# A Mamba-2 and attention trunk: the products inside the chunks in one run per group, and dt's projection in plain fp32 column tiles

## The chip, the cores and the metric

One core of one Trainium2 chip runs the whole kernel. The metric is the device time of one execution in microseconds (us). TensorE multiplies matrices, VectorE (DVE), ScalarE (ACT) and GpSimd (POOL) do the elementwise work, and SyncE (SP) issues nearly all transfers.

## The reference

The input is one sequence of 512 tokens with 1024 features, in float32. Two layers follow each other, then a final RMS norm.

```
# layer 1: Mamba-2 mixer (8 groups of 4 heads, head dim 64, state 128)
h = rms_norm(x, norm_g);  zxbcdt = h @ w_in          # z 2048, x/B/C 4096, dt 32 columns
xbc = silu(causal_depthwise_conv(xbc))               # 4 taps
dt = softplus(dt_raw + dt_bias);  adt = -exp(a_log) * dt
# scan, in chunks:
acs = cumsum(adt);  decay = exp(acs[l] - acs[s]) for s <= l
y_diag = (C B^T * decay) @ (x * dt)                  # the products inside the chunk
y_off  = (C @ state) * exp(acs)                      # what earlier chunks left
y = y_diag + y_off + d_skip * x
y = group_rms_norm(y * silu(z)) * g;  x = x + y @ w_out
# shared K/V of x; layer 2: differential attention (8 heads, two softmax maps each,
# ALiBi, block-causal mask), gate, out projection, residual; final RMS norm
```

## The kernel before

Everything is float32. The large projections are made of three fp32r products each (high part by high part, high by low, low by high), so that every weight and every activation is first split into a rounded high part (`whi`, `a_hi`: ScalarE) and the rest (`wlo`, `a_lo`: VectorE). Smaller products (the scan, the transposes, attention's weighted sums) are plain fp32, which the trace shows as two TensorE instructions for each product.

The sequence is cut into four chunks of 128 tokens (`NQ = NT = 4`). The mixer goes through the groups g = 0 to 7. For each group `group_proj(g)` makes B, C and x (`pg`, 96 products of 512 columns, then `conv`), and `ssd(g)` does the scan:

- `pcb`: C times B for each chunk, into the one bank of the tag "long"; four VectorE products multiply it into `dec`, the decays of the four heads.
- `psA`, `psB`: the states that the chunks leave (`hst`).
- `pyd`: the products inside the chunks. `pyd{g}_0` holds chunks 0 and 1, `pyd{g}_1` chunks 2 and 3. Each of their 32 products has 64 weight columns (half of a chunk's rows, slices 0:64 and 64:128 of the output) and 64 moving columns. VectorE then adds each half into `dx`, which holds the skip term.
- `po1`, `po2`: what the earlier states give, then the gate with z, the group norm (`rsqrt`), the transposes `pyt`, and the split of y into `yh` and `yl` for the output projection.

TensorE's accumulators come from three rings of banks: "mm" (4 banks, the projections), "ss" (3 banks: psA, psB, pyd, po1, po2, the transposes and ps_dt) and "long" (1 bank: pcb, the 1/rms product, later the attention outputs).

The work is traced in this order: the setup with the first half of z's first tile, the row norm `scales` (the 1/rms of every token, as a column and, by one product of a matrix of ones with diagonals that POOL makes, as a row `ar_row`), dt's projection and softplus, the decays, and then the stream `z0 g0 g1 z1 g2 g3 z2 g4 o0 g5 z3 g6 g7 o1 o2 o3` with `ssd(g)` after each g. In this mixer part a planner at build time orders each engine's instructions, by a list of priorities (those traced earlier first) and its own estimate of times: when the inputs of an instruction are late, later work takes its place. At run time every engine goes through its list in order. An instruction that is recorded while `T.on` (or `V.on`, `A.on`) is set is pinned behind the one traced before it on its engine. From the last output projection on (`last_rows`, then attention) everything is pinned, so the order there is the written one.

`dt` before the change: for each of the 8 blocks of 128 features the 32 weight columns are scaled by the norm's gain and split into a high and a low part (`dw`, written twice side by side, 128 columns), and multiplied with the high and the low part of the input (`hh`, `hl`), 512 tokens at once: 16 fp32r products into `ps_dt`. ScalarE and VectorE add the two halves and lay the four token chunks under each other (`pre`), and VectorE multiplies by `r_row`, the row of 1/rms.

Nearly every TensorE, VectorE and ScalarE instruction is issued through the helper `Ordered.call`, which is why the profile shows L55 for it; the groups are told apart by the names of their tiles.

Of the kernel before, what the change touches and what calls it, by code (L numbers as in the profile page):

```python
# [9 lines left out]
F32 = mybir.dt.float32  # L10
F32R = mybir.dt.float32r
I32 = mybir.dt.int32
AF = mybir.ActivationFunctionType
ALU = mybir.AluOpType
# [3 lines left out]
P = 128  # L18
# [3 lines left out]
KD = D // P  # L22
G = 8
R = 4
HD = 64
H = 32
NQ = 4
# [11 lines left out]
C_GA, C_GK, C_GB, C_GG, C_SG, C_DTB, C_AL, C_CB, C_CW = 0, 8, 16, 24, 40, 41, 42, 43, 75  # L39
# [24 lines left out]
def trunk(ctx, tc, x, x_t, par, w_dt, w_in, w_out, w_kvqg, w_bo, d_skip, lam_qk, fin_g, out):  # L64
    nc = tc.nc
    V, A, T = (Ordered(tc, e) for e in (nc.vector, nc.scalar, nc.tensor))
# [14 lines left out]
    def ss_bank(name):  # L81
        turns[0] += 1
        tag = "mm" if turns[0] % turns[1] >= 3 else "ss"
        return psum.tile([P, 512], F32, tag=tag, name=name, bufs=3 if tag == "ss" else 4)

    def long_bank(name):
        return psum.tile([P, 512], F32, tag="long", name=name)
# [10 lines left out]
    prm = const.tile([P, C_CB], F32, name="prm")  # L98
# [142 lines left out]
    def rsqrt(v, n, tag, bufs=2):  # L241


        y = small.tile([P, n], F32, tag=f"{tag}_y", name=f"{tag}_y", bufs=bufs)
        c = small.tile([P, n], F32, tag=f"{tag}_c", name=f"{tag}_c", bufs=bufs)
        iy = small.tile([P, n], I32, tag=f"{tag}_i", name=f"{tag}_i", bufs=bufs)

        def vyy():
            if n == 1:
                V.scalar_tensor_tensor(out=c, in0=y, scalar=v, in1=y, op0=ALU.mult, op1=ALU.mult)  # L250
            else:
                V.tensor_tensor(out=c, in0=y, in1=v, op=ALU.mult)
                V.tensor_tensor(out=c, in0=c, in1=y, op=ALU.mult)

        V.tensor_scalar(out=iy, in0=v.bitcast(I32), scalar1=1, scalar2=None, op0=ALU.logical_shift_right)
        V.tensor_scalar(out=y.bitcast(I32), in0=iy, scalar1=-1.0, scalar2=float(0x5F3759DF - 2 ** 31), op0=ALU.mult, op1=ALU.add)
        vyy()
        V.scalar_tensor_tensor(out=c, in0=c, scalar=-10.0 / 3.0, in1=c, op0=ALU.add, op1=ALU.mult)
        V.scalar_tensor_tensor(out=y, in0=c, scalar=5.0, in1=y, op0=ALU.add, op1=ALU.mult)
        vyy()  # L260
        V.scalar_tensor_tensor(out=y, in0=c, scalar=-64.0 / 3.0, in1=y, op0=ALU.add, op1=ALU.mult)
        return y
# [39 lines left out]
    def scales(tag, ss):  # L302

        V.tensor_scalar(out=ss, in0=ss, scalar1=ROOT2 / D, scalar2=ROOT2 * EPS, op0=ALU.mult, op1=ALU.add)
        col = res.tile([P, NT], F32, tag="r_col", name=f"{tag}r_col")
        V.tensor_copy(col, rsqrt(ss, NT, "y"))
        w = small.tile([P, NT + 1, P], F32, tag="wide", name=f"{tag}diag", bufs=2)
        GP.memset(w[:, NT], 1.0)
        for t in range(NT):
            GP.tensor_tensor(out=w[:, t], in0=ident, in1=col[:, t:t + 1].to_broadcast([P, P]), op=ALU.mult)  # L310
        ps = long_bank(f"{tag}ps_r")
        T.matmul(ps, lhsT=w[:, NT], rhs=w[:, 0:NT].rearrange("p t n -> p (t n)"), start=True, stop=True)
        row = res.tile([P, S], F32, tag="r_row", name=f"{tag}r_row")
        A.copy(row, ps)
        return col, row
# [14 lines left out]
    def new_h(tag):  # L330
        return [res.tile([P, KD, S], F32R, tag=f"hT_{i}", name=f"{tag}_{i}") for i in ("hi", "lo")]
# [9 lines left out]
    hh, hl = new_h("a")  # L341
# [4 lines left out]
    bp2 = bctx.enter_context(tc.tile_pool(name="bp2", bufs=2))  # L346
# [17 lines left out]
    xt = [bp2.tile([P, 2, S], F32, tag="yl", name=f"xt{i}", bufs=4) for i in range(4)]  # L364
# [27 lines left out]
    for t in range(NT):  # L392
        squares(ss, t)
    r_col, r_row = scales("a", ss)
    V.tensor_scalar(out=sg1, in0=prm[:, C_SG:C_SG + 1], scalar1=0.5 * (1.0 - LAM0), scalar2=None, op0=ALU.mult)
    dtw_raw = sm.tile([P, KD, H], F32, name="dtw_raw")
# [1 line left out]

    dw = bp2.tile([P, KD, 2, 2, H], F32R, tag="yh", name="dw", bufs=4)
    for k in range(KD):
        src = dtw_raw[:, k, :].unsqueeze(1).to_broadcast([P, 2, H])
        gk = prm[:, C_GA + k:C_GA + k + 1]
        A.activation(dw[:, k, :, 0], src, AF.Copy, scale=gk)
        V.scalar_tensor_tensor(out=dw[:, k, :, 1], in0=src, scalar=gk, in1=dw[:, k, :, 0].bitcast(F32), op0=ALU.mult, op1=ALU.subtract)
    ps_dt = ss_bank("ps_dt")
    for k in range(KD):
        w = dw[:, k].rearrange("p a b h -> p (a b h)")
        T.matmul(ps_dt, lhsT=w, rhs=hh[:, k, :], start=k == 0, stop=False)  # L410
        T.matmul(ps_dt, lhsT=w, rhs=hl[:, k, :], start=False, stop=k == KD - 1)

    pre = sm.tile([P, P], F32, name="pre")
    for c in range(NQ):
        sl, hi, lo = (slice(i * H, (i + 1) * H) for i in (c, 0, 1))
        cs = slice(c * P, (c + 1) * P)
        A.copy(pre[sl, :], ps_dt[lo, cs])
        V.tensor_tensor(out=pre[sl, :], in0=ps_dt[hi, cs], in1=pre[sl, :], op=ALU.add)
    for c in range(NQ):
        sl = slice(c * H, (c + 1) * H)  # L420
        V.tensor_tensor(out=pre[sl, :], in0=pre[sl, :], in1=r_row[sl, c * P:(c + 1) * P], op=ALU.mult)
    V.tensor_scalar(out=pre, in0=pre, scalar1=prm[:, C_DTB:C_DTB + 1], scalar2=None, op0=ALU.add)
    e1 = sm.tile([P, P], F32, name="e1")
    A.activation(e1, pre, AF.Abs)
# [136 lines left out]
    def ssd(g):  # L561
        bc, cc, x0, x1 = conv_out.pop(g)
        xc = (x0, x1)
        dec, een, _ = decs.pop(g)
# [3 lines left out]
        for c in range(NQ):  # L568
            cs = slice(c * P, (c + 1) * P)
# [8 lines left out]
        for j in range(2):  # L578
            pxt = ss_bank(f"pxt{g}_{j}")
            for c in range(NQ):  # L580
# [5 lines left out]
                            in1=dsk[:, h2].unsqueeze(1).unsqueeze(3).to_broadcast([P, NQ, 2, HD]), op=ALU.mult)  # L586
# [6 lines left out]
        hst = bp.tile([P, 3, R, HD], F32, tag="hst", name=f"hst{g}")  # L593
        hsf = hst.rearrange("p c h e -> p c (h e)")
        psA = ss_bank(f"psA{g}")
        for c in range(2):
            T.matmul(psA[:, c * 256:(c + 1) * 256], lhsT=bt[:, c, :], rhs=xe[:, c].rearrange("p h e -> p (h e)"), start=True, stop=True)
        A.copy(hsf[:, 0], psA[:, 0:256])
# [6 lines left out]

        ss4 = small.tile([P, NQ], F32, tag="ss4", name=f"ss4{g}")
        tmp = bp.tile([P, NQ, R, HD], F32, tag="tmp", name=f"tmp{g}")
        pyd = []
        for q in range(2):
            pyd.append(ss_bank(f"pyd{g}_{q}"))  # L610
            for c in (2 * q, 2 * q + 1):
                for h in range(R):
                    o = (c % 2) * 256 + h * HD

                    for r in (slice(0, 64), slice(64, 128)):
                        T.matmul(pyd[q][r, o:o + HD], lhsT=dec[:, h, c, r], rhs=xdt[:, c, h, :], start=True, stop=True)
            dq = dx[:, 2 * q:2 * q + 2].rearrange("p c h e -> p c (h e)")
            V.tensor_tensor(out=dq, in0=pyd[q].rearrange("p (c e) -> p c e", c=2), in1=dq, op=ALU.add)
        if g % 2 and g < G - 1:
# [5 lines left out]
        for c in (2, 3):  # L625
            T.matmul(po2[:, (c - 2) * 256:(c - 1) * 256], lhsT=cc[:, c * P:(c + 1) * P], rhs=hsf[:, c - 1], start=True, stop=True)
        V.tensor_tensor(out=tmp[:, 1], in0=po1[:, 256:512].rearrange("p (h e) -> p h e", e=HD),
                        in1=eacs_tok[:, 1, hs].unsqueeze(2).to_broadcast([P, R, HD]), op=ALU.mult)
        V.tensor_tensor(out=tmp[:, 2:4], in0=po2.rearrange("p (c h e) -> p c h e", h=R, e=HD),
                        in1=eacs_tok[:, 2:4, hs].unsqueeze(3).to_broadcast([P, 2, R, HD]), op=ALU.mult)  # L630
# [12 lines left out]
        yh = bp2.tile([P, 2, S], F32R, tag="yh", name=f"yh{g}", bufs=4)  # L643
# [11 lines left out]
    for g in range(G):  # L655
        until(f"g{g}")
        if g < G - 1:
            ssd(g)
        else:
            with tc.high_priority():  # L660
                ssd(g)
# [3 lines left out]
    hh, hl = new_h("b")  # L665
# [273 lines left out]
    def half(t, n):  # L939
        hs = slice(n * 512, (n + 1) * 512)  # L940
        return x_tok[:, t, hs], fg[:, hs], ot[t][:, hs], out[t * P:(t + 1) * P, hs]
# [59 lines left out]
    h = DH - 1  # L1001
# [59 lines left out]
    y, f, o, dst = half(3, 0)  # L1061
# [71 lines left out]
```

## Time and profile before

| | us |
|---|---|
| median of 3 runs | 729.46 (729.12 to 731.79) |
| profiled execution, its own time | 729.15 |
| its span, first to last instruction | 727.0 |
| TensorE matmul busy | 713.5 (98%) |
| VectorE busy | 528.0 (73%) |
| ScalarE busy | 433.7 (60%) |
| GpSimd busy | 117.7 (16%) |
| granted TensorE clock | 0.998 |

A row of the profile names the line, the engine, the operation, the tile it writes and those it reads, the shape, the count (x32), and the times. "PEld" is the load of weights into TensorE. In the order of time a row gives its start and the time to the end of its last instruction; in the chain of waits each piece has its start and the time that it held up the end. The mixer part lasts until about 440 us, attention from there to the end.

### The profile page before, as it was taken

Reading aid. Unit: us, or ns where it says so; the run is one execution under the profiler, and the core shown is the slowest. Engines: PE = TensorE matmul, PEld = TensorE weight load, DVE = VectorE, ACT = ScalarE, POOL = GpSimd, SP = SyncE. Lnnn points to the kernel's source line nnn. Section 1 sums busy time; section 2 is a strip of 40 time slices with the busy share of each in tenths; the row PEclk is TensorE's granted clock in tenths of the full one; section 3 lists DMA queues with packets and bytes.
Section 4 is the critical chain, followed back from the end, with each engine's and each line's share of the span. In section 5 each row is a group of like instructions: output and inputs, shape, how many; then the busy total and the mean of one; then the engine's idle time right before and its main releaser. Section 6 shows DMA issues by size and latency. Waiting matters only on the chain.

```text
span 727.0 us, 10819 instructions
## 1 busy us (share of the span) xinstructions
PE 713.5 (98%) x3989; PEld 593.1 (82%) x3989; DVE 528.0 (73%) x1202; ACT 433.7 (60%) x965; POOL 117.7 (16%) x158
## 2 busy tenths in 40 slices
PE   9999999999999999999999999999999999999996
PEld 7787888888888888887788869888988898889874
DVE  4688964979479668569995846657667857785886
ACT  5948573654735527527534348667766756756566
POOL 0108241412315024150110101000000000000002
PEclk9999999999999999999999999999999999999999
DMA  8634313314133231231122310331221131122003
GB/s 302 233 131 162 116 59 117 117 58 175 58 117 116 95 137 60 91 142 59 59 70 105 116 59 9 117 115 59 94 82 58 59 117 59 59 90 85 29 1 115
DMA packets 12916, 70.86 MB, mean 97 GB/s; under 512 B 1728, under 2 KB 2496, under 8 KB 5312
## 3 DMA queue, kind: packets, MB, share of 16 engines
q1 hardware_dynamic: 12576, 69.90, 26.5%
q8 instruction: 31, 0.51, 0.3%
q10 hardware_dynamic: 288, 0.28, 0.1%
q14 instruction: 21, 0.17, 0.1%
HBM read 68.02 MB, written 2.16 MB: 97 GB/s over the span
## 4 chain that ended last, share of the span: by engine, by line
PE 90%; DVE 7%; ACT 1%; issue 1%; POOL 0%; ACTq 0%; DVEq 0%; POOLq 0%
PE pg L55 21%; PE po L55 14%; PE pz L55 12%; PE pt L55 7%; PE pv L55 6%; PE pq L55 6%; PE pk L55 6%; PE pb L55 3%; PE sc L55 3%; PE pyd L55 2%; PE pc L55 2%; DVE wlo L55 2%; DVE xc L55 2%; PE pyt L55 1%; PE pxt L55 1%; PE psA L55 1%
## 5 line engine op out<-in xcount | busy, mean ns | idle before, releaser
L55 DVE SCALAR_TENSOR_TENSOR wlo<-raw,prm,whi 128x512 fp32r<-128x512 f32 (+1 forms) x256 | 150.4, 633 | 52.7 <-ACT whi L55 51.3
L55 ACT ACTIVATE whi<-raw,prm 128x512 fp32r<-128x512 f32 (+1 forms) x256 | 136.8, 606 | 81.4 <-PE pg L55 30.1
L55 PE MATMUL pg<-a_hi,whi 128*128 128x512 f32 x256 | 103.3, 404 | 1.5 <-DVE y_c L55 1.5
L55 PE MATMUL pg<-a_hi,wlo 128*128 128x512 f32 x256 | 102.3, 402 | 0.0
L55 PE MATMUL pg<-a_lo,whi 128*128 128x512 f32 x256 | 102.3, 400 | 0.0
L55 DVE SCALAR_TENSOR_TENSOR xc<-pg,prc,xc 128x511 f32<-128x511 f32 (+2 forms) x96 | 69.6, 738 | 4.8 <-ACT xc L55 4.4
L55 PEld LDWEIGHTS pg<-a_hi,whi 128*128 128x128 f32 x256 | 48.1, 188 | 13.1 <-issue 1.9
L55 PEld LDWEIGHTS pg<-a_hi,wlo 128*128 128x128 f32 x256 | 48.1, 188 | 11.0
L55 PEld LDWEIGHTS pg<-a_lo,whi 128*128 128x128 f32 x256 | 48.1, 188 | 10.7
L55 PE MATMUL po<-whi,yh 128*128 128x512 f32 x128 | 51.4, 402 | 1.5 <-DVE xc L55 0.8
L55 PE MATMUL po<-wlo,yh 128*128 128x512 f32 x128 | 51.1, 399 | 0.0
L55 PE MATMUL po<-whi,yl 128*128 128x512 f32 x128 | 50.4, 398 | 0.0
L55 PE MATMUL pz<-wlo,a_hi 128*128 128x512 f32 x128 | 50.3, 399 | 0.0
L55 PE MATMUL pz<-whi,a_lo 128*128 128x512 f32 x128 | 49.8, 398 | 0.0
L55 PE MATMUL pz<-whi,a_hi 128*128 128x512 f32 x128 | 49.6, 401 | 0.0
L971 POOL TENSOR_TENSOR ot<-ot,fg 128x512 f32<-128x512 f32 x4 | 5.1, 1289 | 256.9 <-ACT ot L55 256.9
L55 ACT ACTIVATE s<-s,mx 128x128 f32<-128x128 f32 (+3 forms) x64 | 35.5, 556 | 9.6 <-DVE mx L55 9.1
L55 ACT ACTIVATE xc<-pg,prc 128x512 f32<-128x512 f32 x32 | 24.6, 773 | 26.6 <-DVE pg L55 26.5
L589 POOL TENSOR_TENSOR xe<-xdt,tok 128x256 f32<-128x256 f32 x24 | 17.3, 749 | 139.6 <-DVE xdt L55 139.6
L55 DVE CUSTOM_DVE_ANT_0 s<-sc,bias 128x128 f32<-128x128 f32 (+3 forms) x64 | 29.4, 488 | 12.2 <-PE sc L55 11.7
L55 ACT ACTIVATE xc<-xc 128x512 f32<-128x512 f32 x32 | 20.0, 629 | 28.3 <-DVE xc L55 28.2
L55 PE MATMUL pv<-whi,b_hi 128*128 128x256 f32 x128 | 36.6, 286 | 0.0
(243 smaller groups left out, 1719.7 us busy)
## 6 DMA issues: line engine op xcount, KB each, us to landing
raw<-in_w_in SPq DMA_DIRECT2D x23, 1024.0 KB, 4.8
raw<-in_w_kvqg SPq DMA_DIRECT2D x16, 1024.0 KB, 4.8
dec<-acs_d SPq DMA_DIRECT2D x8, 1024.0 KB, 4.8
raw<-in_w_out SPq DMA_DIRECT2D x8, 1024.0 KB, 4.8
raw<-in_w_bo SPq DMA_DIRECT2D x4, 1024.0 KB, 4.8
x_tok<-in_x SPq DMA_DIRECT2D x4, 512.0 KB, 9.3
out<-ot SPq DMA_DIRECT2D x7, 256.0 KB, 2.4
raw<-in_w_in SPq DMA_DIRECT2D x4, 256.0 KB, 5.8
```

Of the source, the lines that this page charges most:

```text
L55: i = op(*args, **kw)
L589: GP.tensor_tensor(out=xe[:, c], in0=xdt[:, c], in1=toe_tok[:, c, hs].unsqueeze(2).to_broadcast([P, R, HD]), op=ALU.mult)
L971: GP.tensor_tensor(out=o, in0=o, in1=f, op=ALU.mult)
```

## The change

There are two parts.

In `ssd(g)`, `T.on` is set from psA to the end of pyd, so that psA, psB and the 64 products of pyd keep their order. The second half's accumulator is taken from "long" instead of "ss". The second half is computed first, each chunk's heads in reverse, and the two VectorE adds come after both halves in the trace.

For dt, the raw weights are scaled by the gain in one VectorE product (128x256, in place), and multiplied in plain fp32 with the unsplit input `xt`: for each of the 8 feature blocks four products, one for each token chunk, with 32 weight columns and 128 moving columns, each into its own 32 rows of `ps_dt`. So the chunks come out under each other, and the halves need not be added. The 1/rms product and these 32 products are pinned in this order.

```diff
         ps = long_bank(f"{tag}ps_r")
+        T.on = True
         T.matmul(ps, lhsT=w[:, NT], rhs=w[:, 0:NT].rearrange("p t n -> p (t n)"), start=True, stop=True)
+        T.on = False
...
-    dw = bp2.tile([P, KD, 2, 2, H], F32R, tag="yh", name="dw", bufs=4)
+
+    V.tensor_tensor(out=dtw_raw, in0=dtw_raw, in1=prm[:, C_GA:C_GA + KD].unsqueeze(2).to_broadcast([P, KD, H]), op=ALU.mult)
+    ps_dt = ss_bank("ps_dt")
+    T.on = True
     for k in range(KD):
-        src = dtw_raw[:, k, :].unsqueeze(1).to_broadcast([P, 2, H])
-        gk = prm[:, C_GA + k:C_GA + k + 1]
-        A.activation(dw[:, k, :, 0], src, AF.Copy, scale=gk)
-        V.scalar_tensor_tensor(out=dw[:, k, :, 1], in0=src, scalar=gk, in1=dw[:, k, :, 0].bitcast(F32), op0=ALU.mult, op1=ALU.subtract)
-    ps_dt = ss_bank("ps_dt")
-    for k in range(KD):
-        w = dw[:, k].rearrange("p a b h -> p (a b h)")
-        T.matmul(ps_dt, lhsT=w, rhs=hh[:, k, :], start=k == 0, stop=False)
-        T.matmul(ps_dt, lhsT=w, rhs=hl[:, k, :], start=False, stop=k == KD - 1)
-
+        for c in range(NQ):
+            T.matmul(ps_dt[c * H:(c + 1) * H, 0:P], lhsT=dtw_raw[:, k, :], rhs=xt[k // 2][:, k % 2, c * P:(c + 1) * P],
+                     start=k == 0, stop=k == KD - 1)
+    T.on = False
     pre = sm.tile([P, P], F32, name="pre")
     for c in range(NQ):
-        sl, hi, lo = (slice(i * H, (i + 1) * H) for i in (c, 0, 1))
-        cs = slice(c * P, (c + 1) * P)
-        A.copy(pre[sl, :], ps_dt[lo, cs])
-        V.tensor_tensor(out=pre[sl, :], in0=ps_dt[hi, cs], in1=pre[sl, :], op=ALU.add)
-    for c in range(NQ):
         sl = slice(c * H, (c + 1) * H)
-        V.tensor_tensor(out=pre[sl, :], in0=pre[sl, :], in1=r_row[sl, c * P:(c + 1) * P], op=ALU.mult)
+        V.tensor_tensor(out=pre[sl, :], in0=ps_dt[sl, 0:P], in1=r_row[sl, c * P:(c + 1) * P], op=ALU.mult)
...
         psA = ss_bank(f"psA{g}")
+        T.on = True
...
-        pyd = []
-        for q in range(2):
-            pyd.append(ss_bank(f"pyd{g}_{q}"))
+
+        pyd = [ss_bank(f"pyd{g}_0"), long_bank(f"pyd{g}_1")]
+        for q in (1, 0):
             for c in (2 * q, 2 * q + 1):
-                for h in range(R):
+                for h in reversed(range(R)):
                     o = (c % 2) * 256 + h * HD
 
                     for r in (slice(0, 64), slice(64, 128)):
                         T.matmul(pyd[q][r, o:o + HD], lhsT=dec[:, h, c, r], rhs=xdt[:, c, h, :], start=True, stop=True)
+        T.on = False
+        for q in range(2):
             dq = dx[:, 2 * q:2 * q + 2].rearrange("p c h e -> p c (h e)")
             V.tensor_tensor(out=dq, in0=pyd[q].rearrange("p (c e) -> p c e", c=2), in1=dq, op=ALU.add)
```

## The prediction

> **What bounds the kernel now.** I read the page first: its engine lines and the chain that ended last. Then the busy time by stretches, to find where TensorE waits. Then TensorE's instructions in order of time around one group's products, and the first 36 us of every engine.
>
> ```profile
> span 727.0 us, 10819 instructions
> PE 713.5 (98%) x3989; PEld 593.1 (82%) x3989; DVE 528.0 (73%) x1202; ACT 433.7 (60%) x965; POOL 117.7 (16%) x158
> PE 90%; DVE 7%; ACT 1%; issue 1%; POOL 0%; ACTq 0%; DVEq 0%; POOLq 0%
> ```
>
> TensorE is busy 98% of the span and carries 90% of the chain, so what leaves TensorE's queue leaves the end time, as long as no new wait opens. The stretches tell where real waits lie (columns: stretch, its length, then busy time and instructions of PE, PEld, DVE, ACT, POOL, the clock, the DMA share, GB/s):
>
> ```profile
> 27.00:33.00 6.00, 6.00 (x26) 4.54 (x25) 3.11 (x6) 5.58 (x13) 2.93 (x4) 1.00 0.41 124
> 33.00:49.00 16.00, 16.00 (x70) 12.85 (x70) 13.21 (x33) 8.98 (x17) 0.00 (x0) 1.00 0.27 92
> 49.00:70.00 21.00, 20.39 (x97) 16.37 (x96) 18.20 (x27) 15.49 (x19) 15.04 (x18) 1.00 0.52 200
> 310.00:320.00 10.00, 10.00 (x78) 8.09 (x74) 5.28 (x11) 2.76 (x6) 2.91 (x4) 1.00 0.33 112
> 315.00:330.00 15.00, 14.09 (x61) 11.14 (x60) 13.73 (x23) 6.83 (x14) 9.79 (x12) 1.00 0.40 141
> 330.00:350.00 20.00, 19.38 (x97) 16.14 (x98) 16.61 (x29) 14.59 (x23) 0.00 (x0) 1.00 0.16 53
> 350.00:365.00 15.00, 14.17 (x88) 11.17 (x87) 15.00 (x24) 7.00 (x11) 3.46 (x5) 1.00 0.28 84
> 410.00:425.00 15.00, 13.71 (x61) 10.28 (x60) 11.88 (x31) 7.40 (x20) 2.32 (x3) 1.00 0.39 140
> 480.00:700.00 220.00, 220.00 (x1260) 191.05 (x1259) 161.07 (x484) 145.83 (x419) 0.00 (x0) 1.00 0.20 70
> ```
>
> From 480 to 700 us there is no wait, and the order there is pinned by hand, so the attention part only moves with its start. In the mixer part TensorE waits 0.61 + 0.91 + 0.62 + 0.83 = 2.97 us in four stretches, and 1.29 us at its tail, 410 to 425.
>
> **The products inside the chunks (pyd).** The run of group 0's first half, and its neighbours, in order of time (start, length to the end of the last one):
>
> ```profile
> 77.29 0.59 PE L55 MATMUL psA<-xe,bt 128*128 128x256 f32 x2
> 77.72 0.59 PE L55 MATMUL psB<-xe,bt 128*128 128x256 f32 x2
> 78.24 1.15 PE L55 MATMUL pyd<-xdt,dec 128*64 128x64 f32 x32
> 79.33 0.50 PE L55 MATMUL pg<-a_hi,whi 128*128 128x512 f32 x1
> 79.66 0.40 PE L55 MATMUL pg<-a_lo,whi 128*128 128x512 f32 x1
> 79.89 0.40 PE L55 MATMUL pg<-a_hi,wlo 128*128 128x512 f32 x1
> ...
> 78.24 1.01 PEld L55 LDWEIGHTS pyd<-xdt,dec 128*64 128x64 f32 x32 [0.33 <-PE psA L55]
> ```
>
> Products of 512 columns last 0.40 us in the rows but start 0.23 us apart, so a pause below 0.17 us shows in no busy share. A pair of 256-column passes takes 0.43 us (77.29 to 77.72), so psB is through at 78.15. The next run is back in step when its second product starts, so its first would have started undisturbed at 79.66 - 0.23 = 79.43. The run thus costs 1.28 us of TensorE. Its inner pace comes from the weight loads: first to last takes 1.01 us less one load of 0.138 (the next fence), 0.87 us, for 15 steps between 16 pairs, 0.058 us a pair and 0.93 us for 16. The other 0.35 us are entering and leaving the half-width form: about 0.1 before it, the first load that nothing covers, and 0.1 twice behind it. There are two such runs in each of the 8 groups:
>
> ```profile
> L55 PEld LDWEIGHTS pyd<-xdt,dec x512: 132/138/138, 78.2 to 408.3; 128*64 128x64 f32 x171
> 402.18 0.59 PE L55 MATMUL psB<-xe,bt 128*128 128x256 f32 x2
> 402.70 1.15 PE L55 MATMUL pyd<-xdt,dec 128*64 128x64 f32 x32
> ...
> 404.12 0.39 PE L55 MATMUL po<-whi,yh 128*128 128x512 f32 x1
> ...
> 407.46 1.15 PE L55 MATMUL pyd<-xdt,dec 128*64 128x64 f32 x32
> ```
>
> Group 7's first run costs the same (402.18 + 0.43 = 402.61 to 404.12 - 0.23 = 403.89: 1.28), and its second comes 4.8 us later. One run of 64 pays the 0.35 once: 8 x 0.35 = **-2.8 us**. Bounds: nothing, if something still lands between the halves, to -2.8. I take -2.8, because a run of 32, once its inputs are there, is one piece in these rows, and both halves now have their inputs at the same time: by the code the second half waited for one of three "ss" banks, which psA, psB and the first half hold, and it takes the long bank instead. That bank was pcb's, which the four dec products have read before any pyd can start. Reversing the heads makes the run wait for the last of the four; the rows show pyd right behind psB, so that costs nothing. Pinning psA, psB, pyd in order costs nothing either, since they stand so already.
>
> What the later half releases: its add into dx, then the gate, the group norm and the transposes of y. Groups 0 to 6 have other TensorE work behind them. The tail has none:
>
> ```profile
> 407.53 1.11 PE pyd L55 x32
> 408.66 2.74 DVE wlo L55 x4
> 411.40 0.60 DVE dx L55
> 421.52 1.54 PE pyt L55 x7
> ```
>
> This is the chain that ended last: group 7's second half, its add, the norm and the transposes pyt, while TensorE runs out of other work and loses the 1.29 us. Merged, that half ends near 404.8 in these times, 3.8 us earlier, and I expect the whole 1.29 to be covered: **-1.3 us** (0, if the weight splits wlo and whi still stand ahead of the add and the norm; the nearest row for that is the 2.74 above, which leaves 1 us of the 3.8). Next to be late would be the loads and splits of the following weights, which this change does not touch.
>
> **dt's projection.** What goes and what takes its place:
>
> ```profile
> 27.01 3.73 PE ps_dt L55 x16
> 26.59 3.34 POOL L310 TENSOR_TENSOR adiag<-ident,ar_col 128x128 f32<-128x128 f32 x4 [3.94 <-DVE ar_col L55]
> 365.47 0.89 PE pcb L55 x8
> 35.34 0.29 DVE L55 TENSOR_SCALAR pre<-pre,prm 128x128 f32<-128x128 f32 x1
> L55 DVE TENSOR_TENSOR tmp<-po,tok 128x256 f32<-128x256 f32 x8 | 3.3, 414 | 0.0
> ```
>
> Out go 16 products of 3.73 us. In come 8 x 4 plain products with 32 weight columns and 128 moving ones. A plain fp32 product is two passes here (4 pcb products are x8), and a pass of 128 columns takes 0.89 / 8 = 0.111 us. That makes 64 passes. pyd shows how narrow tiles overlap: 64 columns should take 0.055 us a pass, and a pair of them takes 0.058, so two tiles run fully side by side, passes included. If four do likewise: 16 rounds x 0.111 = 1.78, plus 0.35 for the change of form, 2.13. If only two: 32 x 0.111 + 0.35 = 3.9. If none: 64 x 0.111 + 0.35 = 7.5. I take 2.13, nearest to the pyd rows, **-1.6 us**; the ends are -1.95 (no change of form to pay) and +3.7.
>
> The Trainium skill ("TensorEngine Tiling (Array Packing)", Performance Considerations) gives 4x for 32 weight columns, which is the 2.13. It also ("TensorE: Matmul & The Clock Gate", Part 3) has matmuls start and end strictly in program order. By that the second pass of a tile holds up the next tile, the overlap stays at two tiles, and dt takes the 3.9; no run here has four tiles.
>
> Beside TensorE: ACT loses 8 scalings and 4 copies, DVE 8 corrections and 4 adds; DVE gains one product of about 0.41 us (the 128x256 row). TensorE is full from 27 to 49 us, so this is worth nothing directly. The new wait: dt stands behind the 1/rms product, and that waits for POOL's diagonals, done at 26.59 + 3.34 = 29.93. TensorE no longer has dt to run from 26.84; it has ten pz products (2.3 us, to 29.2) and then group 0's pg. pg's first weights are split by then:
>
> ```profile
> 25.73 2.57 ACT L55 ACTIVATE whi<-raw,prm 128x512 fp32r<-128x512 f32 x4 [0.40 <-DMA raw<-in_w_in]
> 26.49 3.17 DVE L55 SCALAR_TENSOR_TENSOR wlo<-raw,prm,whi 128x512 fp32r<-128x512 f32 x4
> ```
>
> So I cost the wait at nothing; if the product is queued right behind pz it is 0.7 us, and everything behind it in TensorE's queue waits too. dt's own chain is no later: r near 30, dt to 33, four products of 0.3 us, against pre's last step at 35.34 now. No DMA changes place on SP; the input blocks that dt now reads are kept until about 33 us, and their buffers are wanted again only for group 0's y, after its whole scan.
>
> **The sum** against the profiled execution: span 727.0, its own time 729.15, so 2.15 around it; the median of the runs is 729.46, 0.3 above. 729.15 - 2.8 - 1.6 - 1.3 = **723.5**. The four waits of 2.97 us elsewhere I leave as they are: the order before 430 us is largely made by the planner, every engine's order will be drawn anew, and these waits can go (-3) or double (+3).
>
> **Rivals.**
> *Four tiles run as two* (10%): 723.5 + 1.8 = 725.3. For it: pyd shows two side by side and no row shows four. Against it: in pyd the second pass of one tile does not hold up the other's first (0.058 a pair, not 0.11).
> *VectorE eats it* (18%): it is busy all of 350 to 365 and 13.73 of 15 from 315. If the mixer's second half runs at its pace, what TensorE gained ahead of 365 us (1.6 + 6 x 0.35 = 3.7) turns into waits there: 727.2. Against it: from 310 to 320 VectorE is idle 4.7 of 10 us, so an earlier TensorE feeds it earlier.
> *The run is still cut* (6%): the pin keeps an order, but lets unpinned products in between. Then pyd gives nothing, and the tail's half stays where it is: 729.15 - 1.6 = 727.6.
> *The long bank holds back the next group* (5%, the one that ends slower): pcb of the next group now waits until VectorE has added this group's second half. This matters only where groups stand close, 6 and 7. pcb of 7 is at 365.47 (above), and VectorE's adds there come late:
>
> ```profile
> 357.46 1.15 PE L55 MATMUL pyd<-xdt,dec 128*64 128x64 f32 x32
> 362.87 0.67 DVE L55 TENSOR_TENSOR dx<-pyd,dx 128x512 f32<-128x512 f32 x1
> 366.36 1.08 PE pyd L55 x32
> ```
>
> The first half's add comes 5.4 us after its run starts. If the second half's, and with it pcb of 7, slips by the 8.9 us that this half waited for a bank until now, and the tail covers none of it: 723.5 + 1.3 + 8.9 = 733.7. It decides from a slip of 4.4 us, the 2.8 and the 1.6. Against it: 362.87 is still ahead of 365.47.
> *The waits shrink too* (8%): 720.5.
>
> **Numbers.** The forecast has 53%, its own range 721.5 to 725.5. No change is what lies within 0.5%, 3.65 us, about what a measurement of this kernel can tell. Below 725.8 are the forecast (51 of 53), the shrunken waits (8), most of the two-tile case (8) and a little of VectorE's: 0.68. Above 733.1 is most of the long-bank case: 0.04. Without 2 in 10 the range is 720.8 to 727.5.
>
> **What would show it.** pyd: 8 runs of x64, near 2.2 us each, where 16 of x32 stood. dt: 64 passes in about 2.1 us behind the 1/rms product; near 3.9 or 7.5 for the rivals. TensorE's wait at the tail below 0.3 us, and group 7's adds less than 1 us apart on TensorE's side. VectorE idle about 4 us from 310 to 320 as now; near none means that it has become the bound. pcb of group 7 no later than before, against the end of group 7's pg. The forecast is wrong if the four waits, drawn anew, come to over 5 us.

## The result, and the profile after

The changed kernel takes 721.06 us (median of 4 runs, 720.31 to 721.43) against 730.0 for the kernel before on the same chip: a ratio of 0.9873, 95% interval 0.9852 to 0.9895. On the 729.46 of the prediction that is 720.2, a gain of 9.3 us where 6.0 were forecast, just outside the range. The profiled execution took 720.89 us, 1.8 of it around its span. Two of the six executions of `e_nopin` below were slow ones (1007 and 4034 us) and are left out of its figures.

The page's head of the changed kernel, and then the stretches with the same columns as before:

```profile
span 719.1 us, 10908 instructions
PE 709.1 (99%) x4037; PEld 591.5 (82%) x4037; DVE 521.0 (72%) x1191; ACT 430.3 (60%) x953; POOL 112.8 (16%) x158
```

```profile
49.00:70.00 21.00, 20.78 (x100) 16.77 (x99) 20.41 (x30) 16.96 (x20) 15.54 (x19) 1.00 0.52 201
315.00:330.00 15.00, 15.00 (x66) 12.13 (x65) 13.20 (x21) 9.83 (x17) 8.22 (x11) 1.00 0.28 100
330.00:350.00 20.00, 20.00 (x101) 16.59 (x100) 16.81 (x35) 12.45 (x23) 0.00 (x0) 1.00 0.28 105
350.00:365.00 15.00, 15.00 (x125) 12.49 (x124) 15.00 (x25) 6.55 (x13) 3.00 (x5) 1.00 0.21 72
410.00:425.00 15.00, 14.35 (x62) 10.54 (x61) 6.96 (x20) 6.84 (x18) 0.00 (x0) 1.00 0.19 70
```

TensorE is now busy without a break from 315 to 365 us, where it had waited twice. The prediction counts four waits, one for each stretch, but there were three: its 0.91 and 0.62 us are the two ends of one wait across 330 us, which in the kernel before stands in this row, in order of time:

```profile
330.62 0.47 PE L55 MATMUL pg<-a_hi,whi 128*128 128x512 f32 x1 [1.53 <-DVE y_c L55]
```

Of the 2.97 us only 0.22 is left, in 49 to 70, and of the tail's 1.29 us 0.65. VectorE is busy all of 350 to 365, as before, and yet TensorE does not wait for it there.

TensorE's instructions in order of time, around dt and around group 0's products:

```profile
29.35 1.02 PE L55 MATMUL aps_r<-adiag 128*128 128x512 f32 x2
30.30 1.95 PE L55 MATMUL ps_dt<-xt,dtw_raw 128*32 128x128 f32 x64
32.19 0.50 PE L55 MATMUL pg<-a_hi,whi 128*128 128x512 f32 x1
...
75.66 0.59 PE L55 MATMUL psB<-xe,bt 128*128 128x256 f32 x2
76.19 2.08 PE L55 MATMUL pyd<-xdt,dec 128*64 128x64 f32 x64
78.20 0.50 PE L55 MATMUL pg<-a_hi,wlo 128*128 128x512 f32 x1
78.54 0.40 PE L55 MATMUL pg<-a_hi,whi 128*128 128x512 f32 x1
```

Group 0's 64 products are one run. Measured as in the prediction, from the end of psB (75.66 + 0.43 = 76.09) to the undisturbed start of the next (78.54 - 0.23 = 78.31), it costs 2.22 us. All eight groups look so: 17.71 us together, where the 16 half runs cost 20.47. dt's 64 passes cost 2.08 in the same measure, and pg begins at 32.19, 1.55 earlier than in the kernel before:

```profile
33.74 0.40 PE L55 MATMUL pg<-a_hi,whi 128*128 128x512 f32 x1
```

The list of TensorE's waits in the kernel before (columns: the waiting tile, the releaser, total, times, longest), without two on `pc` of 0.5 and 0.4 at the very end, which both kernels have:

```profile
PE pg L55 <- DVE y_c L55: 1.5, 1, 1.5
PE warm L55 <- POOL ident masks.py:199: 1.5, 1, 1.5
PE po L55 <- DVE xc L55: 0.8, 1, 0.8
PE pyt L55 <- ACT tmp L55: 0.7, 1, 0.7
PE pxt L55 <- ACT xc L55: 0.6, 1, 0.6
PE po L55 <- ACT yh L55: 0.6, 1, 0.6
```

The same list of the changed kernel:

```profile
PE warm L55 <- POOL ident masks.py:199: 1.5, 1, 1.5
PE po L55 <- ACT yh L55: 0.6, 1, 0.6
...
PE pxt L55 <- ACT xc L55: 0.2, 1, 0.2
```

The waits of `pg` on `y_c`, of `po` on `xc` and of `pyt` on `tmp` are gone. So the span's 7.9 us (727.0 to 719.1) come to: pyd 2.76, dt 1.55, the waits ahead of the tail 2.75 (2.97 to 0.22), the tail 0.64, together 7.7.

### The profile page after: what moved, and what is told of

It reads as the page before. It is cut to its first block, busy times and chain, and to the rows that moved or that the text cites. A ratio compares the mean times of both kernels' runs of the same rounds, so it can differ in the third digit from the quotient of the medians.

```text
span 719.1 us, 10908 instructions
## 1 busy us (share of the span) xinstructions
PE 709.1 (99%) x4037; PEld 591.5 (82%) x4037; DVE 521.0 (72%) x1191; ACT 430.3 (60%) x953; POOL 112.8 (16%) x158
## 4 chain that ended last, share of the span: by engine, by line
PE 94%; DVE 2%; ACT 2%; issue 0%; POOL 0%; ACTq 0%; POOLq 0%
PE pg L55 23%; PE po L55 16%; PE pz L55 13%; PE pt L55 7%; PE pq L55 6%; PE pv L55 6%; PE pk L55 6%; PE pb L55 3%; PE sc L55 3%; PE pyd L55 2%; PE pc L55 2%; PE pyt L55 1%; PE pxt L55 1%; PE psA L55 1%; PE pcb L55 1%; PE warm L55 1%
## 5 line engine op out<-in xcount | busy, mean ns | idle before, releaser
L583 POOL TENSOR_TENSOR xe<-xdt,tok 128x256 f32<-128x256 f32 x24 | 14.1, 615 | 161.2 <-DVE xdt L55 161.2
L547 POOL TENSOR_TENSOR dec<-dec,tok 128x512 f32<-128x512 f32 x32 | 36.0, 1156 | 0.6
```

The lines of the kernel that those rows point to most:

```text
L547: GP.tensor_tensor(out=dec[:, h], in0=dec[:, h], in1=acs_tok[:, :, R * g + h].unsqueeze(2).to_broadcast([P, NQ, P]), op=ALU.subtract)
L583: GP.tensor_tensor(out=xe[:, c], in0=xdt[:, c], in1=toe_tok[:, c, hs].unsqueeze(2).to_broadcast([P, R, HD]), op=ALU.mult)
```

## The experiments

**One part at a time.** `e_dt` is the kernel before with the dt part of the change alone, `e_ssd` the kernel before with the part in `ssd(g)` alone; the diffs are the two halves of the diff above. The experiments ran on several chips, the kernel before on each of them beside them, with medians from 729.7 to 731.1 us; so a difference of 1 us between runs of two chips says little.

> dt's part alone (plain fp32 column tiles, pinned behind the 1/rms product); ssd as before. Theory A, the waits in the mixer go because the second half of pyd comes earlier: here they stay, 4.3 us of shown TensorE idle time between 49 and 430 us, and only dt's own 1.65 us of TensorE time are won: about 1.6 us less than before (0.998). Theory B, dt's part makes the waits go (it frees VectorE and ScalarE early and moves everything): about 1.6 + 2.8 = 4.4 us less (0.994). Theory C, any change redraws the order and the waits fall as they will: between 1.4 us more and 5 us less, with waits at other places than before.

Measured: 731.48 us, ratio 1.0015 (1.0001 to 1.0029). The dt run costs 2.08 us as in the changed kernel, and the products of the first groups come 2.4 to 2.9 us earlier than before, up to 217 us. Then the lead is lost in waits, from its list:

```profile
PE pg L55 <- DVE y_c L55: 1.9, 1, 1.9
PE po L55 <- DVE x_tok L55: 1.9, 1, 1.9
```

The second is new, and ends at 232.1 us. What VectorE and GpSimd do ahead of it, in order of time:

```profile
223.31 5.22 POOL L546 TENSOR_TENSOR dec<-dec,tok 128x512 f32<-128x512 f32 x4
...
223.43 1.54 DVE L55 SCALAR_TENSOR_TENSOR wlo<-raw,prm,whi 128x512 fp32r<-128x512 f32 x1
224.89 1.27 DVE L55 TENSOR_TENSOR dx<-dx,zs 128x256 f32<-128x256 f32 x1
226.08 2.99 DVE L55 SCALAR_TENSOR_TENSOR wlo<-raw,prm,whi 128x512 fp32r<-128x512 f32 x2
```

A `wlo` took 1.54 us and a `dx` by zs 1.27, beside GpSimd's four subtractions for the decays. Just ahead of them, at 222.43 and 223.09, one of each took 0.74 and 0.42.

> ssd's part alone (pins, long bank, second half first); dt as before. Theory A: 8 x 0.35 = 2.8 us of TensorE time and the waits (2.7 in the middle, 0.7 at the tail): about 6.2 us less than before (0.9915). Theory B: 2.8 and the tail's 0.7: about 3.5 us less (0.995). Theory C: 3.5 us less, give or take 3.

Measured: 722.26 us, 0.9884 (0.9863 to 0.9905). The eight runs of 64 are there, 2.21 us each, and the list is as short: of the mixer's waits only `pxt` (0.8) and `yh` (0.6) remain. So this part brings 7.4 us by the medians, 8.5 by the ratio, and not the 4.1 of my two terms (2.8 and 1.3); dt adds about 1.2 on top of it by the medians (722.26 to 721.06) and by the spans (720.3 to 719.1), though the intervals of the two ratios overlap; alone it gains nothing.

**What the one run needs.** Four kernels take single pieces away or add them:

```diff
 # e_nopin: the changed kernel without the pin in ssd
-        T.on = True          # ahead of psA
-        T.on = False         # behind pyd
 # e_bankonly: the kernel before with the second half in the long bank
-            pyd.append(ss_bank(f"pyd{g}_{q}"))
+            pyd.append(long_bank(f"pyd{g}_{q}") if q else ss_bank(f"pyd{g}_{q}"))
 # e_ssbank: the changed kernel with the second half in an "ss" bank
-        pyd = [ss_bank(f"pyd{g}_0"), long_bank(f"pyd{g}_1")]
+        pyd = [ss_bank(f"pyd{g}_0"), ss_bank(f"pyd{g}_1")]
 # e_natural: the changed kernel with halves and heads in the old order
-        for q in (1, 0):
+        for q in (0, 1):
-                for h in reversed(range(R)):
+                for h in range(R):
```

> The kernel after without the pins in ssd (dt's pins stay). If the planner keeps the run together by itself once bank and order are there: the time of the kernel after (0.987 of before). If the pins matter: up to 8 cuts at 0.35 us, 2.8 us slower than the kernel after (0.991).

Measured: 725.9 us, 0.9935 (0.9896 to 0.9974). The planner cuts the 64 products of the groups into 20 runs, in group 0 into three with psA and psB between them, in order of time:

```profile
73.33 0.34 PE L55 MATMUL pyd<-xdt,dec 128*64 128x64 f32 x4
...
74.22 0.33 PE L55 MATMUL pyd<-xdt,dec 128*64 128x64 f32 x2
...
75.54 1.96 PE L55 MATMUL pyd<-xdt,dec 128*64 128x64 f32 x58
```

Their cost, measured as above, is 22.70 us, 5.0 more than in the changed kernel. The times differ by 4.8 and the spans by 4.4. TensorE's waits are those of the changed kernel but for one of 0.2.

> The kernel before with one edit: the second half of pyd takes the long bank. Not pinned, first half first. If the bank was all that parted the halves: 8 runs of x64 and the same time as ssd's part alone, about 6 us less than before. If the pins or the reversed order are what makes the run: 16 runs still, or 8 with a gap of filled-in products, and at most the waits' share, about 3 us less.

Measured: 732.49 us, 1.0041 (1.0025 to 1.0056). With the bank and no pin there are 29 runs, 26.10 us, 5.6 more than before. Yet the waits on `y_c` and on `xc` that end at 330.6 and 362.4 us in the kernel before are gone here too. What that gives back, the cut runs take, and more: the interval lies above 1.

> The kernel after with the second half's bank taken from the three ss banks again; pins and reversed order stay. The second half is now the first in the run. If pins and order alone make one run of 64: 8 runs and the time of the kernel after (0.987). If the bank matters: the first half, now last, waits for psA's bank as the second did before, its pinned products stand in the queue, and the run is cut in two, with 0.35 us a group or 2.8 us lost (0.991), or TensorE waits in it.

Measured: 729.77 us, 0.9979 (0.9957 to 1.0001). Without the long bank there are 16 runs of 32 again, pin and order or not, and the waits are back: `pg` for `y_c` 2.1, `pyt` for `tmp` 1.6, and one of 0.9 right behind a half run near 167 us. The runs come to 21.42 us with that 0.9, and to 20.5 without it, as before. So bank and pin are needed together: the bank lets the second half follow, the pin keeps others out.

> The changed kernel with the two halves and the heads of the products inside the chunks in their old order (first half first, heads forward), still pinned and still with the long bank. Prediction's step: the reversed order costs nothing and gives nothing of itself; then 8 runs of x64 of 2.2 us each stay and the time is 721.1 give or take 1. If the reverse is needed, because a run that starts with head 0 waits inside for the fourth dec product, the footprint of some runs rises above 2.2 (up to 0.5 us each, the length of one dec product) and the time goes to 722 to 725.

Measured: 723.28 us, 0.9899 (0.9872 to 0.9927). All eight runs stay uncut with the same inner 1.86 us, so the reversed order is worth nothing to the run itself. The time is still 2 us worse, though the intervals of the two ratios overlap. The span is 1.8 longer, and the waits list names 1.0 for `pg` on `v` at 326 us and 0.8 for `pz` on `a_hi`. VectorE and GpSimd ahead of 326:

```profile
314.52 5.42 POOL L547 TENSOR_TENSOR dec<-dec,tok 128x512 f32<-128x512 f32 x4
...
314.97 5.52 DVE L55 SCALAR_TENSOR_TENSOR wlo<-raw,prm,whi 128x512 fp32r<-128x512 f32 x4
```

Four `wlo` took 3.17 us in the prediction's row and take 5.52 here, beside the decays' subtractions. The old order costs nothing inside the runs; what it changes is the order that the planner draws, in which the decays meet four weight corrections. That this makes the wait at 326 is argued from the rows.

**dt's tiles.** Two kernels, both made from the changed one:

```diff
 # e_serial: tile by tile
-    for k in range(KD):
-        for c in range(NQ):
+    for c in range(NQ):
+        for k in range(KD):
 # e_dtfree: no pin on the 1/rms product and on dt
-    T.on = True
-    T.on = False
```

> The changed kernel with one difference: dt's 32 products are queued tile by tile (all 8 feature blocks of chunk 0, then chunk 1, and so on) instead of the four tiles in turn. All other orders on all engines stay the same. If tiles run side by side only where neighbours in the queue belong to different tiles, the 64 passes go one after the other: 64 x 0.109 + 0.35 = 7.3 us in place of 2.08, and the time rises by about 5.2, to 726.3. If the side by side running needs only that the tiles differ somewhere ahead in the queue, it stays at 2.1 us and 721.1. If the second pass of a product held up the next tile, the order of the passes in the changed kernel would have shown it already; here it makes no difference.

Measured: 724.38 us, 0.9909 (0.9887 to 0.9931), 3.3 above the changed kernel. The dt run costs 6.08 us instead of 2.08; of the 4.0 more, 0.5 is covered by an earlier start of the 1/rms product (28.87 us) and 0.2 by the missing wait of `pxt`:

```profile
29.82 5.95 PE L55 MATMUL ps_dt<-xt,dtw_raw 128*32 128x128 f32 x64
```

Inside a tile the passes start 0.109 us apart. Only at the three changes of tile do some run side by side; there the steps are 6, 103, 30, 79, 30, 79 and 30 ns, which saves 0.4 us each, and 7.3 - 3 x 0.4 = 6.1. In the changed kernel four passes start within 20 ns, and the next four 0.109 later. So passes run side by side only with neighbours in the queue, a few passes ahead at most.

> The changed kernel without the pin on the 1/rms product and dt. The planner then puts dt ahead of the last 15 products of pz, with the 1/rms product in the middle of dt's run. If the pin is what keeps TensorE from waiting for POOL's diagonals, TensorE now waits in the queue at the 1/rms product: it comes there about 15 x 0.23 = 3.4 us earlier than in the changed kernel (29.35), so near 26, while the diagonals were done at 28.3: a wait of about 2 us, the run cut in two for another 0.35, and a time near 723.5. If the pin is only for show, the time stays at 721.1. The waits further back are drawn anew in either case (up to 3 us).

Measured: 724.39 us, 0.9912 (0.989 to 0.9934). The wait is where it was expected, but half as long, and the dt run is cut:

```profile
25.86 1.30 PE L55 MATMUL ps_dt<-xt,dtw_raw 128*32 128x128 f32 x40
28.24 1.12 PE L55 MATMUL aps_r<-adiag 128*128 128x512 f32 x2 [1.08 <-POOL adiag L310]
29.30 0.86 PE L55 MATMUL ps_dt<-xt,dtw_raw 128*32 128x128 f32 x24
```

Other waits of a newly drawn order come with it (`pxt` 1.5, `po` 0.7, `pz` 0.7, `pyt` 0.5). Together the list holds more than the 3.3 us, and what each of them costs is not parted here. In the changed kernel the pin holds this product behind pz, and it does not wait.

**GpSimd beside VectorE.** Three kernels leave out GpSimd's 32 subtractions in `decays`, so their decays are no longer relative to the source token: `e_nopool` from the kernel before, `e_dt_nopool` from `e_dt`, `e_after_nopool` from the changed kernel.

```diff
-                GP.tensor_tensor(out=dec[:, h], in0=dec[:, h], in1=acs_tok[...], op=ALU.subtract)
```

> The kernel before, leaving out GpSimd's 32 subtractions in the decays (34.9 us of GpSimd; the decays are then not relative to the source token). TensorE's work is the same. Theory P, GpSimd's long products slow VectorE's work in SBUF and so make TensorE wait near 227 and 327 us: the wait near 327 us (1.5 us) goes, VectorE's 128x4 operations take 0.16 us everywhere, and the time falls by 1.5 to 3 us (0.996 to 0.998). Theory R, the waits are an accident of the planned order: their sum changes by up to 3 us either way, and VectorE's small operations are long elsewhere.

> dt's part alone, again without GpSimd's 32 subtractions. Theory P: the 1.9 us wait on x_tok near 228 us and the one near 326 us are gone, so dt's gain comes through here: about 1.6 us less than the same leaving-out without dt's part, 3 to 5 us less than before (0.993 to 0.996). Theory R: as before, within 1 us (1.000), with waits elsewhere.

> The kernel after without GpSimd's 32 subtractions. Theory P: the kernel after has no small VectorE operation beside GpSimd's long ones any more, and TensorE waits 0.2 us in the middle, so little is left to win: 0 to 1 us less than the kernel after (0.985 to 0.988 of before). Theory R: within 3 us either way of the kernel after.

Measured: 732.15 (1.0015, 0.9999 to 1.0031), 732.9 (1.002, 1.0006 to 1.0033) and 728.35 (0.9956, 0.9941 to 0.9971). None gets faster by it. The waits that I looked at do shrink: the one of `pg` that the expectations place near 327 us, from 1.5 to 0.7 in `e_nopool`, where `y_i` and `y_y` of the same norm take 0.17 us each (0.97 and 0.98 in the kernel before, shown further down); and the one for `x_tok` is gone in `e_dt_nopool`. But the planner, with less work on GpSimd, draws another order and opens waits elsewhere: `pxt` waits 3.2 us for `xc` near 68 us in two of the three, and 1.9 in `e_nopool`. An edit to the mixer part cannot separate the two theories, since it moves everything. So the next one adds GpSimd's work where no order changes, beside attention:

```diff
+    for i in range(100):
+        GP.tensor_tensor(out=tok.rearrange("p a c h -> p a (c h)"), in0=dist.rearrange("p (t n) -> p t n", n=P),
+                         in1=ident[:, 0:NQ].unsqueeze(2).to_broadcast([P, NQ, P]), op=ALU.subtract)
     lq = cp2.tile([P, 4, 64], F32, tag="gt", name="lq", bufs=3)
```

> The changed kernel with 100 operations of GpSimd added that nothing reads (128x512 subtractions from SBUF into a table that is no longer needed, like the decays' own), beside the attention part, from about 448 us on. No other engine's order changes. If GpSimd's operations stretch VectorE's, then in the 100 us that they last the 128x4 operations of the heads' norm go from 0.16 us to between 0.4 and 1.0, and the weight corrections wlo (128x256, 0.48 us, all in SBUF) to about 0.8, while operations that read an accumulator (k, q_lo, gt) keep their 0.68; VectorE, busy 14 of 20 us there, then comes near to full and the time rises by 0 to 5 us. If the decays and the long 128x4 operations only fell together by chance, every VectorE row keeps its time and the kernel stays at 721.1.

Measured: 747.58 us, 1.0228 (1.0205 to 1.0251): 27.5 us above the changed kernel on the same chip (720.1, `after_again` below), more than five times what I had thought the most. The view by tile gives minimum, median and maximum in ns. First `wlo` of the changed kernel in this stretch, then `wlo`, the added operations and `q_lo` of this one:

```profile
L55 DVE SCALAR_TENSOR_TENSOR wlo<-raw,prm,whi x56: 473/479/486, 448.8 to 529.0; 128x256 fp32r<-128x256 f32 x56
```

```profile
L55 DVE SCALAR_TENSOR_TENSOR wlo<-raw,prm,whi x56: 481/1256/1354, 447.7 to 559.9; 128x256 fp32r<-128x256 f32 x56
L896 POOL TENSOR_TENSOR tok<-dist,ident x100: 1040/1101/1571, 451.7 to 568.1; 128x512 f32<-128x512 f32 x100
L55 DVE TENSOR_TENSOR q_lo<-pq,q x6: 674/689/695, 470.4 to 527.7; 64x512 fp32r<-64x512 f32 x6
```

The weight corrections, whose operands are all in SBUF, go from 0.48 to 1.26 us. `q_lo`, which reads an accumulator, keeps its 0.69. In order of time:

```profile
469.42 12.73 POOL L896 TENSOR_TENSOR tok<-dist,ident 128x512 f32<-128x512 f32 x11
473.03 2.31 DVE L55 SCALAR_TENSOR_TENSOR wlo<-raw,prm,whi 128x256 fp32r<-128x256 f32 x2
```

11 operations of GpSimd in 12.73 us and two `wlo` in 2.31 are 1.16 us apiece on either side: the two engines take turns, one VectorE operation for each of GpSimd's. The Trainium skill ("SBUF — State Buffer", section "SBUF: two separate sides") says that VectorE operations with two SBUF inputs share a port pair with GpSimd, held by one of them for a whole instruction; these rows agree with it as to the turns. GpSimd's own operations are hardly longer for them, 1.10 us in the median against 1.04 at least, and how long either engine holds the pair the rows do not show.

So the stretching is caused by GpSimd's work and does not need the mixer. What lengthens the time is, besides the waits that follow from it, the clock: behind the longest of them, products of 512 columns that had been 0.23 us apart come 0.43 apart, in order of time, and by stretches the granted clock (third column from the end) reads 0.50 and then 0.97:

```profile
484.64 0.48 PE L55 MATMUL pt<-ident,s 128*128 128x128 f32 x1 [3.68 <-DVE s L55]
...
485.77 0.63 PE L55 MATMUL pt<-b_hi,wlo 128*128 128x512 f32 x1
486.20 0.63 PE L55 MATMUL pt<-b_hi,whi 128*128 128x512 f32 x1
```

```profile
485.00:490.00 5.00, 5.00 (x13) 3.88 (x13) 3.48 (x7) 2.50 (x7) 4.69 (x5) 0.50 0.33 134
490.00:495.00 5.00, 5.00 (x25) 4.22 (x24) 3.56 (x8) 4.14 (x11) 4.61 (x6) 0.97 0.00 0
```

The Trainium skill ("TensorE: Matmul & The Clock Gate", Part 1) has the clock halved behind an idle window of about 3.4 us, until a busy one has passed; the wait of 3.68 and the 5 us at 0.50 agree with it.

**The tail.** What is left of it stands behind the splits of v0's weights (`whi`, `wlo` 128x256, eight each), which the planner puts between the pieces of group 7's norm. `e_late` leaves them to the last rows; `e_tail` queues them behind group 7's last `yh` and `yl`; `after_again` is the changed kernel beside it.

```diff
 # e_late
-        if seg == ("o", 3, 0):
-            for piece in loaded.pop(i + 2)():
-                lay(piece)
 # e_tail, where last_y holds group 7's copy into yh and its subtraction into yl
-            for piece in loaded.pop(i + 2)():
-                lay(piece)
+            with tc.issue_after(last_y[0].ins), tc.issue_after(last_y[1].ins):
+                for piece in loaded.pop(i + 2)():
+                    lay(piece)
```

> The changed kernel without the splitting of v0's weights ahead of group 7's norm: the eight whi (3.31 us on ScalarE) and eight wlo (some 3.6 us on VectorE) are laid out later, among the last output projection's rows. If they are what still holds the tail (the norm takes from 407.66 to 412.81, where without them it needs about 2.6 us), pyt moves from 413.63 to about 411, the wait of 0.57 us at 415.84 goes, and the time is 0.6 below the changed kernel, 720.5. If the wait there has another cause, it stays at 721.1; if the later splits come too late for the attention part, TensorE waits near 434 us and the time rises by 1 to 3.

Measured: 723.11 us, 0.9894 (0.9875 to 0.9913), 2 us worse. The norm does end 2.7 us earlier (tmp from 410.35 instead of 413.07), but TensorE's queue has pyt behind the same products of the output projection, so pyt starts at 413.29 and only its length shrinks, from 1.64 to 1.04. The wait for `yh` stays: it is the copy of pyt itself, with nothing queued to cover it. And the moved splits stand in front of the next row norm: its list has a new wait of 2.4 us, `btp` for ScalarE's `xn`.

> The changed kernel with v0's splits (8 whi, 8 wlo) queued behind group 7's last yh and yl instead of between the pieces of its norm. TensorE's order and everything behind 421 us stay the same, other than in the kernel that paced these splits through the last rows. If the splits hold up the tail, the transposes pyt take 1.04 us instead of 1.64 (their inputs are there), the first po behind them comes 0.7 to 0.9 earlier, nothing is late at the attention part, and the time is 0.7 below the changed kernel. If the splits are then late for v0 or delay the squares behind x_tok at 421, the gain is given back and the time is the same or up to 1 more.

> The changed kernel once more, beside e_tail on the same chip, so that half a microsecond can be told: 721.1 by the first measurement, ratio 0.987 to before.

Measured: `e_tail` 720.25 (719.9 to 721.3), 0.9849 (0.9829 to 0.9868); `after_again` 720.1 (719.88 to 720.4), 0.9848 (0.9828 to 0.9868). In the profiled execution of `e_tail` the tail is shorter as expected: TensorE needs 0.7 us less from group 7's psB to the first `btp` than in the changed kernel. The times show none of it. The front differs by more from run to run: the 1/rms product starts at 29.35, 28.62 and 29.45 us in the changed kernel, its repetition and `e_tail`, and group 0's psB 1.1 later in `e_tail` than in the first. So no version found here is measurably better than the change as it stands.

## Why the prediction was right or wrong

*pyd, -2.8:* right, 2.76, by the mechanism given: one change of form, 0.35 us, is paid per run, and `e_nopin` shows the price from the other side (12 more runs, 5.0 us, 0.42 each).

*Pinning costs nothing, "since they stand so already":* right of the changed kernel and incomplete as a reason. Without the pin the long bank makes the planner cut the runs (`e_bankonly`, `e_nopin`); the pin is worth 4.4 us by the spans and 4.8 by the medians.

*dt, -1.6:* right, 1.65 in TensorE's time and 1.55 at pg's start. Four tiles run side by side; the rival with two fell. The starts do come in program order, 7 ns apart; what was wrong is the step from there, that the second pass of a tile holds up the next tile. `e_serial` shows on what the overlap hangs. That no wait opened behind POOL's diagonals was in part luck: they took 1.93 us instead of 3.34 and were done at 28.27, ahead of the product at 29.35; with 3.34 they would have been done at 29.68, and 0.3 us of wait would have been left. The four `wlo` beside them began at 27.09 instead of 26.49 us; in `e_tail`, where they began at 28.20, the diagonals took 1.47.

*The tail, -1.3:* the mechanism held, the size was off: 0.64. What is left is the copy of pyt, 0.57, for which I had no term. The splits that I named as the limit are there too: they hold up pyt by another 0.6 (1.64 against 1.04), in pauses too short for the busy share.

*"The four waits ... I leave as they are":* this is the step that failed, a term put at nothing because the planner might move it either way. The waits fell from 2.97 us to 0.22, and with that 2.75 the forecast would have been 720.75. I had put this case at 8%. The rows in which the cause could have been read were there. In the kernel before, in order of time, GpSimd's subtractions and group 5's norm, just ahead of the wait of 1.5 us:

```profile
320.94 4.92 POOL L553 TENSOR_TENSOR dec<-dec,tok 128x512 f32<-128x512 f32 x4
...
323.89 0.97 DVE L55 TENSOR_SCALAR y_i<-v 128x4 int32<-128x4 int32 x1
324.90 0.98 DVE L55 TENSOR_SCALAR y_y<-y_i 128x4 int32<-128x4 int32 x1
```

The same in the changed kernel:

```profile
317.38 4.08 POOL L547 TENSOR_TENSOR dec<-dec,tok 128x512 f32<-128x512 f32 x4
...
334.55 0.16 DVE L55 TENSOR_SCALAR y_i<-v 128x4 int32<-128x4 int32 x1
335.33 0.16 DVE L55 TENSOR_SCALAR y_y<-y_i 128x4 int32<-128x4 int32 x1
```

An operation on four columns that takes 0.16 us took 0.97 while the decays ran. VectorE's `xc`, which read the accumulators of `pg`, stand behind these in its queue, and TensorE's wait ends among them (the list names `y_c`). In the changed kernel the decays are over before the norm begins. They run beside `xc` and `pg`, which read accumulators and keep their times, and the subtractions themselves take 4.08 us instead of 4.92. It is so in all the kernels: of the 80 operations on 128x4 in the eight norms, those over 0.3 us number 14 before, 13 in `e_dt` and 22 in `e_ssbank`, each beside GpSimd's work on `dec`, and none in any kernel with the long bank. Every kernel with the second half in "ss" and GpSimd's work whole has the wait that ends near 331 us (before 1.5, `e_dt` 1.9, `e_ssbank` 2.1). Of those with the long bank and GpSimd's work whole, only `e_natural` has one near there, where the decays fall beside `wlo`.

*VectorE eats it, 18%:* fell. VectorE is as full from 350 to 365 as before, and from 310 to 320 it is idle for 1.6 us and not for the 4 that I had named as the sign; yet TensorE does not wait. But `e_dt` is what this rival described, at another place: 2.4 to 2.9 us of lead, all lost again.

*The run is still cut,* and *the long bank holds back the next group:* neither came; pcb of group 7 opens no wait.

What stays open: `e_ssd`, `e_bankonly` and `e_ssbank` show that the long bank removes the wait of 1.5 us, `e_pool_att` shows the contention, and the traces show where it fell. But the meetings of the two engines in the mixer part were never changed by themselves. For the wait of 1.5 us the rows account: two operations are each 0.8 us too long, and in `e_nopool`, where they are not, 0.7 of wait is left. The 0.8 on `xc` is gone in all three, in `e_ssbank` without the bank too, and why is not shown. The 0.6 of `pxt` is still there in these three (0.7 to 0.8); it is absent in `e_dt` and reads 0.2 and 0.4 in two executions of the changed kernel, so it goes with dt's part or with chance.

## What to carry to other kernels

A short wait on a row of trivial length is a place to look, not noise to leave as it is: ask why a 128x4 operation takes 0.97 us in one place and 0.16 in another. Where a planner orders the engines, an edit that frees time early moves every later meeting of two engines, and a part that does what it should (dt, 1.6 us of TensorE) can still bring nothing when a wait behind it takes the gain. And narrow products belong together on TensorE: a bank that lets them follow and a pin that keeps others out are worth something only as a pair.

## What the runs showed of the hardware

Four tiles of 32 weight columns in plain fp32 run fully side by side (a round of four passes in 0.109 us, starts 7 ns apart), but only if neighbours in TensorE's queue belong to different tiles: tile by tile the same 64 passes take 6.08 us instead of 2.08. A run of narrow products among full ones costs about 0.35 us on top of its passes, wherever it is cut. GpSimd's 128x512 operations slow VectorE's weight corrections, all in SBUF, from 0.48 to 1.26 us by turns, and leave those that read an accumulator alone; not every operation in SBUF is slowed (a reciprocal on 128x1 kept its 0.15 us). And a wait of 3.7 us on TensorE costs more than itself: the products behind it ran at half their pace for some 5 us, and so the 15.8 us in which TensorE stood idle from 448 to 570 us, with a granted clock of 0.90 in the mean, lengthened the span by 28.
